# The second half's norm listed between the early up products, and the last down product ending by 256 tokens

## The chip, the cores and the metric

The kernel runs on one core of one Trainium2 chip, as one program. The metric is the device time of that program in microseconds (us): 2468.15 us as the median of 3 runs before the change (2466.43 to 2470.87). Engines are named as in the profile: PE is TensorE (matrix products), PEld its weight loads, DVE is VectorE, ACT is ScalarE, SP is the engine that issues all transfers here.

## The reference

Two decoder layers on 1024 tokens of width 1024, then a norm. All that matters here is the second part of a layer and the end:

```
for layer in range(DEPTH):
    ...
    x = x + mixed @ w_out[layer]
    h = rms_norm(x, norm_mlp[layer])
    x = x + jnp.square(jax.nn.relu(h @ w_up[layer])) @ w_down[layer]
return rms_norm(x, norm_final)
```

`rms_norm` divides each token by the root of the mean of its 1024 squares and multiplies by a gain per feature. The hidden width is 4096.

## The kernel before, in words

**Layout.** Activations lie transposed, features on the 128 partitions and tokens along the row: a tile is 128 features by 512 tokens (W), so a layer's x is 8 feature tiles times 2 token halves, `xs[k][hf]`. Q is 256 tokens. Every product is made of three float32r products of a rounded part h and a rest l (`ah`, `al`, `w..h`, `w..l`): ScalarE casts the h part, VectorE subtracts to get the l part (`split`, L316 and L318).

**Up product.** `h @ w_up` is done by Winograd's form of Strassen's scheme over the two feature halves and the two token halves: 7 products in place of 8 for each of 16 groups j of 256 hidden columns. Two of the seven need the first token half alone (`"11"` and `"21"`, operands `b11`, `b21`); the other five need differences of both halves (`"22"`, `"t1"` to `"t4"`, operands `b22`, `bt1` to `bt4`). `norm_up(hf)` norms one half and makes its operands: it saves 8 tiles of x to DRAM (`xm<-x`), sums the squares (`m0sq`; m1 in the second layer), has TensorE add them over the features (`m0ms`, L426 and L427), takes the reciprocal root on ScalarE (`m0rs`), and then, for each of four pairs p of feature tiles, makes the operands. For the second half (hf = 1) a pair costs VectorE two scaled copies (`mt<-x`, L448), four subtractions and five l parts, and ScalarE five casts.

`up_early` does the two first-half products of groups 0 to 9 (EARLY = 10): it splits the group's weights, multiplies, adds the products (`c<-m,psu`), squares the positive part and spills it. `up_rest(j)` does the other five products of such a group, with sums of the weights made on VectorE (`sums_of`: s1 to s4, each split as well); `up_all(j)` does all seven for groups 10 to 15.

**Order.** Nothing is issued in the order of the source. `op` lists each operation with a cost and its buffers, and the listing order is its number; generators that run through `weave` are listed alternately, by the given weights. `Program.order` then plays the list with its own costs: whenever an engine is free in that play, it takes the ready operation of the lowest number whose buffers can be had (not further ahead of the oldest open operation than a bound, 60 us of TensorE work). The order that comes out is fixed, and on the chip each engine works through its own list and waits where an input is late. Buffers are counted: 71 slots for tiles of 512 columns, 8 each for weight parts (`whi`, `wlo`), 4 for raw weights, 8 PSUM banks.

In listing order the second half's norm stands behind all of `up_early`, and `up_rest(0)` behind that norm.

**End of the last layer.** `down` multiplies the hidden tiles by `w_down` in seven products again. The last, `"22"`, is listed with `tail=4`: for j from 0 to 11 the four output tiles q take turns; for the last four j each q is brought to its end in turn (L1407 to L1409, 12 matmuls of 512 columns) and its result added to the second-half tile `xs[q][1]`. `norm_out` then squares the eight tiles, adds them (`finsq`), sums over features on TensorE (`finms`, one plain float32 product by a matrix of ones), takes the root (`finrs`, two ScalarE instructions), and eight times multiplies a tile by gain and root (`y<-x,colt,finrs`, L448) and stores it (L501). A branch of `norm_out` for a width of Q exists: there ScalarE multiplies by the gain beforehand, two tiles share one y of 128x2x256, four VectorE products by the root follow and four stores, with runs of 256 tokens in DRAM.

Of the kernel before, what the change touches and what calls it, by code (L numbers as in the profile page):

```python
# [15 lines left out]
OP = mybir.AluOpType  # L16
# [3 lines left out]
L = 2  # L20
# [4 lines left out]
KT = D // 128  # L25
NH = 2
W = 512
Q = 256
# [17 lines left out]
def weave(*parts):  # L46

    live = [[0, *p] if isinstance(p, tuple) else [0, p, 1] for p in parts]
    while live:
        part = min(live, key=lambda p: p[0] / p[2])  # L50
        part[0] += 1
        if next(part[1], live) is live:
            live.remove(part)
# [18 lines left out]
class Part:  # L72


    def __init__(self, buf, start, stop):
        self.buf, self.start, self.stop = buf, start, stop
        self.writers, self.readers = [], []

    @property
    def t(self):  # L80
# [35 lines left out]
class Program:  # L116
# [9 lines left out]
    def op(self, eng, cost, writes, reads, emit, table=None, join=False):  # L126
        engines = eng if isinstance(eng, dict) else {eng: cost}
        self.ops.append(Op(len(self.ops), engines, list(writes), list(reads), emit, table, join))
# [119 lines left out]
def trunk(ctx: ExitStack, tc: tile.TileContext, xT, wts, cols, trig, toep, lmask, ident_d, out):  # L248
    nc = tc.nc
    V, A, PE = nc.vector, nc.scalar, nc.tensor  # L250
# [15 lines left out]
    op = prog.op  # L266
# [23 lines left out]
    def c_mm(n):  # L290
        return max(107.0, 2.3 + n / 2.4)
# [10 lines left out]
    def tt(dst, a, b, kind, n=W, extra=()):  # L302

        op("DVE", c_tt(n), [dst[0]], [x[0] for x in (a, b) if x[0] is not None] + list(extra),
           lambda e: V.tensor_tensor(dst[1](), a[1](), b[1](), op=kind))  # L305

    def whole(b):
        return b, lambda: b.t
# [171 lines left out]
    def norm_out(xs, t0, width=W):  # L480
        r = rstd(xs[4:] + xs[:4], D, "fin", width=width)
        yield
        if width == Q:
            pairs = []
            for k in range(0, KT, 2):
                y = slot("y", shape=[128, 2, Q])
                for i in range(2):
                    op("ACT", c_act(Q) + 110, [y], [xs[k + i], colt], lambda e, y=y, i=i, k=k + i: A.activation(
                        y[:, i], xs[k].t, AF.Copy, scale=col(C_FIN + k)), join=True)
                pairs.append(y)  # L490
            for k, y in zip(range(0, KT, 2), pairs):
                tt(whole(y), whole(y), (r, lambda: r.t[:, None, :].to_broadcast([128, 2, Q])), OP.mult)
                op("SP", 730.0, [], [y], lambda e, k=k, y=y: nc.sync.dma_start(
                    out[k * 128:(k + 2) * 128, t0:t0 + Q].rearrange("(i p) t -> p i t", i=2), y.t))
                yield
            return
        for k in (4, 5, 6, 7, 0, 1, 2, 3):
            y = slot("y", width=width)
            stt(whole(y), whole(xs[k]), lambda k=k: col(C_FIN + k), whole(r), width)
            op("SP", 730.0, [], [y],  # L500
               lambda e, k=k, y=y: nc.sync.dma_start(out[k * 128:(k + 1) * 128, t0:t0 + width], y.t))  # L501
            yield
# [7 lines left out]
    def load_x(src, k, hf):  # L510
        x = slot(f"x{k}_{hf}")
        i, j = rows(k, hf)
        saved = src and src[k][hf]
        if saved:
            load(x, lambda: x.t, lambda: saved.t, 1 << 18, saved)
        else:
            load(x, lambda: x.t, lambda: xT[i, j], 1 << 18)
        return x
# [16 lines left out]
    xs, hs, rs, xsaved = table(), table(), {}, None  # L535
    first = [Group(j, f"w0h0{j}") for j in range(4)]
# [33 lines left out]
    for l in range(L):  # L570
# [621 lines left out]
        xs = table()  # L1192
# [6 lines left out]
        hf32, xmid = table(), table()  # L1199

        def norm_up(hf):


            for k in range(KT):
                d, x = Buf(f"xm{l}_{k}_{hf}", "dram", [128, W], F32), xs[k][hf]
                load(d, lambda d=d: d.t, lambda x=x: x.t, 1 << 18, x)
                xmid[k][hf] = d
            r = rstd([xs[k][hf] for k in range(KT)], D, f"m{l}", True)
            yield
            for p in range(4):  # L1210
                for k in (p, p + 4):
                    t = hf32[k][hf] = slot("mt")
                    stt(whole(t), whole(xs[k][hf]), lambda c=C_MLP + l * KT + k: col(c), whole(r))
                if hf == 0:
                    bo["11"].append(hilo(hf32[p][0], "b11", p < COUNT["kk"]))
                    bo["21"].append(hilo(hf32[p + 4][0], "b21"))
                else:
                    (b11, b12), (b21, b22) = hf32[p], hf32[p + 4]
                    bo["22"].append(hilo(b22, "b22"))
                    t3 = slot("t3")  # L1220
                    tt(whole(t3), whole(b22), whole(b12), OP.subtract)
                    bo["t3"].append(hilo(t3, "bt3"))
                    tt(whole(b12), whole(b12), whole(b11), OP.subtract)
                    bo["t1"].append(hilo(b12, "bt1"))
                    tt(whole(b22), whole(b22), whole(b12), OP.subtract)
                    bo["t2"].append(hilo(b22, "bt2"))
                    tt(whole(b21), whole(b21), whole(b22), OP.subtract)
                    bo["t4"].append(hilo(b21, "bt4"))
                yield
# [65 lines left out]
        def up_early():  # L1295

            for j in range(EARLY):
                grp = group_up(j)
                m1, c11 = slot("m1"), slot("c11")
                act(m1, product(grp.piece(0), "11", "sc"), AF.Copy)  # L1300
                m1s[j] = m1
                tt(whole(c11), whole(m1), whole(product(grp.piece(1), "21", "gemm")), OP.add)
                relu2(c11)
                spill("11", j, c11)
                yield
# [45 lines left out]
            operands(j, c11, c12, c21, c22)  # L1351

        weave((out_part(0, xs, (1,)), 8), (norm_up(0), 5))
        weave(up_early())
        weave(norm_up(1))
        for j in range(16):
            if j < EARLY:
                up_rest(j)
# [3 lines left out]
        xs = table()  # L1362
# [29 lines left out]
            tt(whole(sums[j]), a12, whole(sums[j]), OP.subtract)  # L1392
            return whole(sums[j])

        def down(n, weight, banks, into, first=True, tail=0):


            def operands(j):
                t = slot("al")
                load(t, lambda t=t: t.t, lambda d=ao[n][j]: d.t, 1 << 18, ao[n][j])  # L1400
                return *hilo(t, "a"), *parts(weight(j), f"w{l}d{n}{j}")

            def step(j, q, th, tl, wh, wl):
                ps = banks[q]

                def emit(e, cs=slice(q * 128, q * 128 + 128)):
                    PE.matmul(ps.t, lhsT=wh[:, cs], rhs=th.t, start=first and j == 0, stop=False, skip_group_check=True)  # L1407
                    PE.matmul(ps.t, lhsT=wh[:, cs], rhs=tl.t, start=False, stop=False, skip_group_check=True)  # L1408
                    PE.matmul(ps.t, lhsT=wl[:, cs], rhs=th.t, start=False, stop=j == 15, skip_group_check=True)  # L1409

                op("PE", 3 * c_mm(W), [ps], [wh, wl, th, tl], emit)
                if j < 15:
                    return
                for half, hf in into:
                    m = 4 * half + q
                    if xs[m][hf] is None:
                        xs[m][hf] = load_x(xmid, m, hf)
                    tt(whole(xs[m][hf]), whole(xs[m][hf]), whole(ps), OP.add)

            together = 16 - tail  # L1420
            for j in range(together):
                have = operands(j)
                for q in range(4):
                    step(j, q, *have)
                yield
            have = [operands(j) for j in range(together, 16)]
            for q in range(4) if tail else ():
                for j in range(together, 16):
                    step(j, q, *have[j - together])
                yield  # L1430

        def banks(*tags):
            return [bank("psd", t) for t in tags]

        some, rest = ("gemm", "gemm", "gemm", "acc"), ("sc", "sc", "tr", "tr")
# [4 lines left out]
        weave(down("t3", w_s3, chain, ((1, 1),), False))  # L1440
        weave(down("t4", lambda j: raw(j, 3, 1, "e")[0], chain, ((1, 0),), False))
        weave(down("21", lambda j: raw(j, 0, 1, "f")[0], banks(*rest), ((0, 0),)))
        final = down("22", w_s4, banks(*some), ((0, 1),), tail=4)
        if l + 1 < L:
            hs, rs, xsaved = table(), {}, table()
            after = [norm_in(l + 1, xs, hf, hs, rs, xsaved) for hf in range(NH)]
            weave((final, 16), (after[0], 9))
            weave(after[1])
            continue
        weave((final, 16), (norm_out([x[0] for x in xs], 0), 9))  # L1450
        weave(norm_out([x[1] for x in xs], W))

    loaded = "ln"
    for o in prog.order():
# [96 lines left out]
```

## Time and profile before

| | us |
|---|---|
| median of 3 runs | 2468.15 |
| profiled execution, time | 2466.34 |
| profiled execution, span of the trace | 2464.6 |
| TensorE busy | 2400.8 (97%) |
| VectorE busy | 1734.3 (70%) |
| ScalarE busy | 1209.8 (49%) |
| mean granted TensorE clock | 0.986 of full |

The span runs from the first to the last instruction of the trace; the program's own time is 1.7 us longer. A busy share says little here, since TensorE is called busy when its matmuls run slowly too; stretches with fewer matmuls per microsecond, or a lower granted clock (PEclk), are where time is lost.

### The profile page before, as it was taken

To read this page: it belongs to the slowest core of one execution; us is meant where nothing else is said; L and a number is where in the kernel's file an instruction comes from. 1 tells how busy PE (TensorE), PEld (TensorE's weight loads), DVE (VectorE), ACT (ScalarE), POOL (GpSimd) and SP (SyncE) were. 2 spreads that over 40 slices of the span, in tenths; PEclk is the share of its full clock that TensorE was granted. 3 is DMA by queue.
4 is the path that set the end of the run, shared out by engine and by line. 5 is a ranking of instruction groups with operands and counts; after the bars stand their busy time and mean duration, and the time that the engine had idled before them with its cause. 6 is when DMAs were issued, how large, how long until landed. Compare 5 with 4: busy or idle time off the path is not lost.

```text
span 2464.6 us, 35165 instructions
## 1 busy us (share of the span) xinstructions
PE 2400.8 (97%) x12522; PEld 2029.6 (82%) x12522; DVE 1734.3 (70%) x3403; ACT 1209.8 (49%) x2365; POOL 0.2 (0%) x4
## 2 busy tenths in 40 slices
PE   9999999999899999999999999999998999999997
PEld 7888898877678888888888989898776888888886
DVE  6366877788688667765744678788778875786565
ACT  7233346665554555444532333576555545554452
POOL 0000000000000000000000000000000000000000
PEclk9999999999899999999999999999998999999998
DMA  4011366843445469656520115668342654786562
GB/s 175 26 57 39 130 208 187 273 130 124 145 178 206 144 218 326 219 185 224 172 81 18 61 52 175 190 210 259 104 163 106 211 187 142 268 304 226 185 224 79
DMA packets 188656, 407.19 MB, mean 165 GB/s; under 512 B 22656, under 2 KB 23488, under 8 KB 188480
## 3 DMA queue, kind: packets, MB, share of 16 engines
q1 hardware_dynamic: 188480, 404.93, 49.0%
q8 instruction: 99, 1.62, 0.3%
q14 instruction: 77, 0.63, 0.1%
HBM read 291.37 MB, written 113.48 MB: 164 GB/s over the span
## 4 chain that ended last, share of the span: by engine, by line
PE 90%; DVE 4%; DMA 4%; ACT 2%; issue 1%; SPq 0%; DVEq 0%; ACTq 0%
PE psd L1409 8%; PE psd L1408 8%; PE psd L1407 8%; PE psu L1258 8%; PE psu L1257 8%; PE psu L1259 8%; PE sc L945 2%; PE pa L698 2%; PE pso L376 2%; PE pso L375 2%; PE pso L377 2%; PE pv L1108 2%; PE psv L400 1%; PE ptr L1095 1%; PE psva L400 1%; PE psv L401 1%
## 5 line engine op out<-in xcount | busy, mean ns | idle before, releaser
L318 DVE TENSOR_TENSOR al<-al,ah 128x512 fp32r<-128x512 f32 x224 | 152.6, 686 | 57.9 <-ACT ah L316 57.0
L316 ACT CAST ah<-al 128x512 fp32r<-128x512 f32 x224 | 137.0, 618 | 104.7 <-DMA al<-a 58.6
L961 ACT ACTIVATE sp<-sp,ls 128x256 f32<-128x256 f32 (+2 forms) x192 | 99.8, 522 | 16.7 <-DVE ls L950 16.3
L950 DVE CUSTOM_DVE_ANT_0 sp<-sc,tpt 128x256 f32<-128x256 f32 (+1 forms) x192 | 83.1, 439 | 32.1 <-PE sc L945 30.7
L945 PE MATMUL sc<-k,hd 128*128 128x256 f32 (+3 forms) x384 | 94.1, 356 | 7.7 <-DVE ls L950 3.5
L1240 ACT ACTIVATE c<-c 128x512 f32<-128x512 f32 x96 | 60.6, 631 | 35.1 <-DVE c L305 35.0
L1257 PE MATMUL psu<-bt3h,s3h 128*128 128x512 f32 x128 | 52.5, 410 | 23.5 <-ACT bt3h L316 21.8
L945 PEld LDWEIGHTS sc<-k,hd 128*128 128x128 f32 x384 | 60.5, 193 | 14.1 <-DVE ls L950 4.9
L316 ACT CAST pth<-ptr 128x512 fp32r<-128x512 f32 (+1 forms) x96 | 51.3, 552 | 39.0 <-PE ptr L1095 37.6
L1241 ACT ACTIVATE c<-c 128x512 f32<-128x512 f32 x108 | 68.3, 633 | 3.4
L318 DVE TENSOR_TENSOR ptl<-ptr,pth 128x512 fp32r<-128x512 f32 (+1 forms) x96 | 60.7, 641 | 10.4 <-ACT pth L316 9.4
L698 PEld LDWEIGHTS pa<-q,k 128*112 128x112 f32 (+3 forms) x512 | 62.0, 184 | 3.4
L698 PE MATMUL pa<-q,k 128*112 128x64 f32 (+3 forms) x512 | 61.2, 262 | 0.0
L305 DVE TENSOR_TENSOR x<-x,psd 128x512 f32<-128x512 f32 x64 | 41.4, 683 | 27.5 <-PE psd L1409 27.4
L1258 PE MATMUL psu<-bt3l,s3h 128*128 128x512 f32 x128 | 52.3, 408 | 2.2 <-DVE bt3l L318 2.2
L1095 PE MATMUL ptr<-ident,sp 128*128 128x128 f32 x352 | 53.6, 277 | 0.4 <-ACT sp L961 0.2
L305 DVE TENSOR_TENSOR x<-x,pso 128x512 f32<-128x512 f32 x64 | 43.4, 682 | 13.6 <-PE pso L377 12.9
L1258 PE MATMUL psu<-bt1l,s1h 128*128 128x512 f32 x128 | 51.8, 405 | 0.0
L1257 PE MATMUL psu<-bt1h,s1h 128*128 128x512 f32 x128 | 51.8, 404 | 0.0
L1259 PE MATMUL psu<-bt1h,s1l 128*128 128x512 f32 x128 | 51.8, 404 | 0.0
L1257 PEld LDWEIGHTS psu<-bt3h,s3h 128*128 128x128 f32 x128 | 24.6, 192 | 32.4 <-ACT bt3h L316 24.9
L1259 PE MATMUL psu<-bt3h,s3l 128*128 128x512 f32 x128 | 51.3, 400 | 0.0
(4978 smaller groups left out, 8097.0 us busy)
## 6 DMA issues: line engine op xcount, KB each, us to landing
al<-a SPq DMA_DIRECT2D x96, 256.0 KB
w0u<-in_wts_dram SPq DMA_DIRECT2D x42, 512.0 KB
w1u<-in_wts_dram SPq DMA_DIRECT2D x42, 512.0 KB
a<-c SPq DMA_DIRECT2D x76, 256.0 KB
al<-a0t SPq DMA_DIRECT2D x64, 256.0 KB
al<-a1t SPq DMA_DIRECT2D x64, 256.0 KB
hd<-q SPq DMA_DIRECT2D x48, 256.0 KB
a0t<-t SPq DMA_DIRECT2D x48, 256.0 KB
```

What stands on the lines that cost most here:

```text
L305: lambda e: V.tensor_tensor(dst[1](), a[1](), b[1](), op=kind))
L316: op("ACT", c_act(n), [hi[0]], [src[0]], lambda e: A.copy(hi[1](), src[1]()), join=join)
L318: lambda e: V.tensor_tensor(lo[1](), src[1](), hi[1]().bitcast(F32), op=OP.subtract), join=join)
L698: PE.matmul(pa[0:128 - b, c * 64:c * 64 + 64], lhsT=k[:, c * 128:c * 128 + 128 - b], rhs=by_half(q)[:, c, :, 1, :], start=True, stop=True)
L945: PE.matmul(ps[:, o:o + w], lhsT=q[:, q0:q0 + 128], rhs=k[:, keys], start=part == 0, stop=part == 1)
L961: op("ACT", c_act(w) + 190, [t, sum_], [t, m], lambda e, t=t, o=o, w=w, m=m, sum_=sum_: A.activation(t[:, o:o + w], t[:, o:o + w], AF.Exp, ...
L1257: PE.matmul(ps.t, lhsT=wh[:, cs], rhs=xh.t, start=first and k == 0, stop=False, skip_group_check=True)
L1258: PE.matmul(ps.t, lhsT=wh[:, cs], rhs=xl.t, start=False, stop=False, skip_group_check=True)
L1259: PE.matmul(ps.t, lhsT=wl[:, cs], rhs=xh.t, start=False, stop=k == 3, skip_group_check=True)
L1407: PE.matmul(ps.t, lhsT=wh[:, cs], rhs=th.t, start=first and j == 0, stop=False, skip_group_check=True)
L1408: PE.matmul(ps.t, lhsT=wh[:, cs], rhs=tl.t, start=False, stop=False, skip_group_check=True)
L1409: PE.matmul(ps.t, lhsT=wl[:, cs], rhs=th.t, start=False, stop=j == 15, skip_group_check=True)
```

## The change

The generator `norm_up(1)` is no longer listed behind `up_early()` but woven with it, in both layers, at weights 5 to 10: the sums of squares come behind group 0, the four pairs behind groups 2, 4, 6 and 8, and group 9 last.

In the last layer, the last four j of the last product are done in two rounds, first the tokens 0 to 255 of the half for all four q, then the tokens 256 to 511. Each round ends in its own additions to x (256 columns), and each round's 256 tokens have their own final norm, by the branch for a width of Q. `Part.of` makes a part of a buffer that has the buffer's earlier writers and readers. The loop over `load_x` finds all tiles loaded already by the first of the seven products.

```diff
+    @classmethod
+    def of(cls, buf, start, stop):
+        part = cls(buf, start, stop)
+        part.writers, part.readers = list(buf.writers), list(buf.readers)
+        return part
...
         weave((out_part(0, xs, (1,)), 8), (norm_up(0), 5))
-        weave(up_early())
-        weave(norm_up(1))
+        weave((up_early(), 10), (norm_up(1), 5))
...
-            def step(j, q, th, tl, wh, wl):
-                ps = banks[q]
+            def step(j, q, th, tl, wh, wl, end=None):
+                ps, ts = banks[q], slice(0, W)
+                if end:
+                    ps, ts = end[q][1], slice(end[q][1].start, end[q][1].stop)
...
+                    PE.matmul(ps.t, lhsT=wh[:, cs], rhs=th.t[:, ts], start=first and j == 0, stop=False, skip_group_check=True)
...
+                if end:
+                    x = end[q][0]
+                    tt(whole(x), whole(x), whole(ps), OP.add, Q)
                     return
...
-            for q in range(4) if tail else ():
-                for j in range(together, 16):
-                    step(j, q, *have[j - together])
-                yield
+            for end in ends if tail else ():
+                if end:
+                    (half, hf), = into
+                    for m in range(KT):
+                        ps = [Part.of(banks[m % 4], end.start, end.stop)] if m // 4 == half else []
+                        xend[end.start].append([Part.of(xs[m][hf], end.start, end.stop), *ps])
+                for q in range(4):
+                    for j in range(together, 16):
+                        step(j, q, *have[j - together], end and xend[end.start][4 * half:4 * half + 4])
+                    yield
...
-        final = down("22", w_s4, banks(*some), ((0, 1),), tail=4)
+        final = down("22", w_s4, banks(*some), ((0, 1),), tail=4, ends=(slice(0, Q), slice(Q, W)) if last else (None,))
...
-        weave(norm_out([x[1] for x in xs], W))
+        for t0 in 0, Q:
+            weave(norm_out([x[0] for x in xend[t0]], W + t0, Q))
```

## Rows read from the trace of the kernel before

**Rows 1.** The page, part 4: the chain that ended last, by engine.
```profile
PE 90%; DVE 4%; DMA 4%; ACT 2%; issue 1%; SPq 0%; DVEq 0%; ACTq 0%
```

**Rows 2.** View of waits, whole run: who waited for whom, total, times, longest.
```profile
PE psu L1257 <- ACT bt3h L316: 21.8, 6, 4.0
```

**Rows 3.** Busy time by stretch; first line names columns; x is instructions.
```profile
core 0: us, PE busy (x) PEld busy (x) DVE busy (x) ACT busy (x) POOL busy (x), PEclk, DMA share, GB/s
614.50:657.20 42.70, 42.66 (x186) 34.43 (x184) 20.94 (x33) 23.79 (x42) 0.00 (x0) 1.00 0.58 203
...
650.00:700.00 50.00, 38.23 (x134) 28.85 (x133) 43.31 (x71) 26.70 (x45) 0.00 (x0) 0.80 0.22 79
700.00:750.00 50.00, 50.00 (x222) 41.40 (x221) 41.56 (x68) 25.52 (x43) 0.00 (x0) 1.00 0.64 232
1865.00:1915.00 50.00, 37.83 (x136) 28.55 (x135) 42.68 (x70) 27.09 (x46) 0.00 (x0) 0.80 0.23 79
```

**Rows 4.** Timeline of TensorE, layer 0, end of `up_early`: start, length, instruction, idle before.
```profile
655.15 0.39 PE L426 MATMUL m0ms<-m0sh,ones_r 128*128 128x512 f32 x1
...
656.77 0.39 PE L1259 MATMUL psu<-b21h,w0u91l 128*128 128x512 f32 x1
661.18 0.79 PE L1257 MATMUL psu<-bt3h,s3h 128*128 128x512 f32 x1 [4.02 <-ACT bt3h L316]
...
669.43 0.63 PE L1257 MATMUL psu<-bt1h,s1h 128*128 128x512 f32 x1
669.86 0.63 PE L1258 MATMUL psu<-bt1l,s1h 128*128 128x512 f32 x1
```

**Rows 5.** Timeline of VectorE, layer 0: `up_early`, then the second half's norm.
```profile
613.72 0.69 DVE L318 TENSOR_TENSOR m0sl<-m0sq,m0sh 128x512 fp32r<-128x512 f32 x1
...
624.95 0.69 DVE L305 TENSOR_TENSOR c<-m,psu 128x512 f32<-128x512 f32 x1 [1.79 <-PE psu L1259]
...
628.00 0.69 DVE L318 TENSOR_TENSOR w0u80l<-w0u,w0u80h 128x512 fp32r<-128x512 f32 x1 [1.75 <-ACT w0u80h L316]
630.48 0.69 DVE L305 TENSOR_TENSOR c<-m,psu 128x512 f32<-128x512 f32 x1 [1.79 <-PE psu L1259]
...
657.81 2.07 DVE L448 SCALAR_TENSOR_TENSOR mt<-x,colt,m0rs 128x512 f32<-128x512 f32 x3
...
663.41 0.68 DVE L305 TENSOR_TENSOR mt<-mt 128x512 f32<-128x512 f32 x1
664.01 0.68 DVE L318 TENSOR_TENSOR bt2l<-mt,bt2h 128x512 fp32r<-128x512 f32 x1
...
684.78 0.68 DVE L318 TENSOR_TENSOR bt4l<-mt,bt4h 128x512 fp32r<-128x512 f32 x1
```

**Rows 6.** Timeline of TensorE, layer 0: where group 3 of `up_early` begins.
```profile
616.46 0.40 PE L1257 MATMUL psu<-b,w0u30h 128*128 128x512 f32 x1
```

**Rows 7.** Timeline of TensorE: matmuls of 256 columns, six from first to last.
```profile
58.88 0.28 PE L400 MATMUL psv<-w0h032h,n_0h 128*128 128x256 f32 x1
...
59.59 0.40 PE L375 MATMUL psq<-n_1h,w0h013h 128*128 128x512 f32 x1
```

**Rows 8.** Groups by line, shapes apart: VectorE at 256 columns (total us, mean ns).
```profile
L305 DVE TENSOR_TENSOR q<-q,tot 128x256 f32<-128x256 f32 x96 | 40.6, 423 | 6.5 <-PE pa L715 6.3
```

**Rows 9.** Timeline of the end, all engines.
```profile
2449.69 0.39 PE L1409 MATMUL psd<-ah,w1d2215l 128*128 128x512 f32 x1
2450.16 1.31 ACT L312 ACTIVATE finsq<-x 128x512 f32<-128x512 f32 x2 [4.13 <-DVE x L305]
2452.36 2.08 PE L432 MATMUL finms<-finsq,ones 128*128 128x512 f32 x2 [2.29 <-DVE finsq L305]
2454.48 0.69 ACT L312 ACTIVATE finrs<-finms,epst 128x512 f32<-128x512 f32 x1 [3.01 <-PE finms L432]
2455.86 5.39 DVE L448 SCALAR_TENSOR_TENSOR y<-x,colt,finrs 128x512 f32<-128x512 f32 x8 [3.55 <-ACT finrs L312]
2456.64 4.97 SPq L501 DMA_DIRECT2D out_dram<-y  x8
```

More of the change, by code (lines that the diff above doesn't have):

```diff
@@ L1393, in w_s4, with down @@
             return whole(sums[j])
-        def down(n, weight, banks, into, first=True, tail=0):
+        def down(n, weight, banks, into, first=True, tail=0, ends=(None,)):
             def operands(j):
@@ L1401, in operands @@
                 return *hilo(t, "a"), *parts(weight(j), f"w{l}d{n}{j}")
-            def step(j, q, th, tl, wh, wl):
-                ps = banks[q]
+            def step(j, q, th, tl, wh, wl, end=None):
+                ps, ts = banks[q], slice(0, W)
+                if end:
+                    ps, ts = end[q][1], slice(end[q][1].start, end[q][1].stop)
                 def emit(e, cs=slice(q * 128, q * 128 + 128)):
[L1407 to L1411, printed above, removed]
+                    PE.matmul(ps.t, lhsT=wh[:, cs], rhs=th.t[:, ts], start=first and j == 0, stop=False, skip_group_check=True)
+                    PE.matmul(ps.t, lhsT=wh[:, cs], rhs=tl.t[:, ts], start=False, stop=False, skip_group_check=True)
+                    PE.matmul(ps.t, lhsT=wl[:, cs], rhs=th.t[:, ts], start=False, stop=j == 15, skip_group_check=True)
+                op("PE", 3 * c_mm(ts.stop - ts.start), [ps], [wh, wl, th, tl], emit)
                 if j < 15:
+                    return
+                if end:
+                    x = end[q][0]
+                    tt(whole(x), whole(x), whole(ps), OP.add, Q)
                     return
@@ L1442, in trunk @@
         weave(down("21", lambda j: raw(j, 0, 1, "f")[0], banks(*rest), ((0, 0),)))
-        final = down("22", w_s4, banks(*some), ((0, 1),), tail=4)
-        if l + 1 < L:
+        xend = {0: [], Q: []}
+        last = l + 1 == L
+        if last:
+            for m in range(4):
+                if xs[m][1] is None:
+                    xs[m][1] = load_x(xmid, m, 1)
+        final = down("22", w_s4, banks(*some), ((0, 1),), tail=4, ends=(slice(0, Q), slice(Q, W)) if last else (None,))
+        if not last:
             hs, rs, xsaved = table(), {}, table()
```

## The prediction, made before the change was run

> **What bounds the kernel now.** I read the chain of waits first: 90% of it is TensorE [rows 1], so time is won only where TensorE stands still or runs slowly. The view of waits then says where: its largest own wait is for ScalarE's `bt3h`, 21.8 us in 6 waits [rows 2]; these are operands of the second half's norm. The table of stretches shows the full price: from 700 to 750 TensorE starts 222 matmuls in 50 us, one per 0.225 us; from 650 to 700 it starts 134, from 1865 to 1915 136 [rows 3]. Missing are 88 and 86, so 19.8 + 19.4 = 39.2 us over the two layers. This is more than the waits because the granted clock in these stretches is 0.80 of full [rows 3]: after the 4.02 us gap matmuls follow each other at 0.43 us (669.43 to 669.86) [rows 4], the 1.2 GHz level, half the other.
>
> The timelines say why. The squares of the second half are ready when `m0sl` ends at 614.4 [rows 5], but `m0ms` starts at 655.15 [rows 4]: its number stands behind all early products, and TensorE always has one of those. VectorE starts the norm's pairs at 657.81 and ends at 685.46 [rows 5], while TensorE has nothing else it may do. And in the 42.7 us before, VectorE was busy for 20.9 and ScalarE for 23.8 [rows 3].
>
> **The change, part by part.** *Step 1: the norm moves.* `m0ms` now has a number behind group 0 and is taken as soon as its input is there. Two matmuls, two ScalarE instructions and eight stores of x move with it; the stores wait only for x, which is long ready, and no compute waits for them. Price nothing; were the 8 stores to hold SP's queue, weights would come late, but splits run three groups ahead of their use.
>
> *Step 2: does VectorE have room?* The norm's work from 657.81 to 685.46 is 44 instructions with one foreign one of 0.60 between: 27.0 us, or 6.75 per pair (instructions start every 0.60, 663.41 to 664.01) [rows 5]. An early group lasts 5.53 us on TensorE (624.95 to 630.48) and costs VectorE one addition and two splits [rows 5], 1.8 us. So in the woven part, two groups and one pair are 3.6 + 6.75 = 10.35 us of VectorE against 11.06 of TensorE: 94%. It fits, barely. The idle time from 614.5 to 657.2 is 42.7 - 20.9 = 21.8 us [rows 3], against 27.0 wanted; the missing 5 us come out of the weight sums of `up_rest(0)` and `(1)`, which VectorE now does ahead in this stretch and which move behind the norm. A group of `up_rest` is the next customer; from 700 to 750 VectorE is busy 41.6 of 50 [rows 3], so it has 17% to catch up with. ScalarE: 23.8 us plus 20 casts of some 0.62 are 36 of 42.7: no bound.
>
> *Step 3: what is late next.* Two places. First, the opening: once the root is there all four pairs are ready at once, and pair 0 stands ahead of the splits of group 3, which TensorE reaches at 616.46 [rows 6]. The root comes between 611 and 616 (before, `m0sl` began at 613.72 [rows 5] with the nine splits of groups 1 to 5, 0.60 each, ahead of it that now stand behind; 655.15 to 657.81 is the way from `m0ms` to the first copy [rows 4, 5]). So group 3's splits wait for between nothing and a pair, 6.75 us; I take 2 us of standstill. Second, the change to `up_rest(0)`: nine VectorE instructions (sums and splits, 5.4 us) are wanted there and some 6 us are left for them after the last pair: I take no wait. A standstill of some 2 us can cost as much again: `finms`, after 2.29 us without work, takes 2.08 us for two matmuls [rows 9], a slow level; 15 matmuls at 0.43 instead of 0.225 are 3.1 us. So I leave 5 us per layer standing of 19.6, with ends of 0 (no wait at all) and 12 (the opening's full pair, a slow spell and 2 us at the transition). Gain: 39.2 - 10 = 29.2 us, ends 39.2 and 15.
>
> The Trainium skill ("TensorE: Matmul & The Clock Gate", section on the 16 sub-arrays, at its queue depths) says that ScalarE and VectorE take their instructions strictly first in, first out. By it a pair's late instruction holds every split listed behind it, also those whose inputs are there. No row of before shows the price, since the norm stands behind all splits there; what it would do is the last rival below.
>
> *Step 4: 256 columns in the last product.* 48 matmuls of 512 columns become 96 of 256. At 256 columns six take 0.71 us (58.88 to 59.59) [rows 7], 0.118 each, weights loaded for each as here: 96 x 0.118 - 48 x 0.226 = +0.5 us.
>
> *Step 5: the end.* Before, from the start of the last matmul (2449.69) to the span's end (2464.6) it is 14.9 us, of which the eight last products on VectorE take 5.39 and begin only at 2455.86; the last store is issued by 2461.61 and 3.0 us remain [rows 9]. After, counted from the last matmul's start: the first 256 tokens' squares are summed already, but their `finms` has a higher number than the second round's matmuls and goes behind them, at 0.1, for about 0.5 (half of it would be 1.04 at the slow level [rows 9]); two root instructions of 0.42 (the row of 256 columns [rows 8], taken for ScalarE as well): 1.45. Four products of 128x512 at 0.60, 0.08 for the last's length: 4.0. In between the last x tile is added and squared (2.0 at most), but its addition to the sum has the higher number, so VectorE takes it after those four: 4.4. Then `finms` at the slow level 1.04, the root 0.85, four products 2.5: 8.8; and from there 3.35 us as before (2461.25 to 2464.6): 12.2. That is 2.7 less than 14.9; with step 4, 2.2 us gained. If the sum's addition goes first, the second chain runs beside the first and 2.4 us more are gained (4.6). If a store in runs of half the length took twice the time, four stores at 0.62 each (4.97 us for 8 [rows 9]) cost 2.5 more: 0.3 lost. I take 2.2.
>
> *Sum.* The profiled execution took 2466.34 (span 2464.6 and 1.7 around it): 2466.3 - 29.2 - 2.2 = 2434.9. The median of the runs is 1.8 above that execution, so I give 2437.
>
> **Rivals.** *A, all of it goes:* no standstill stays in either layer and the end gains 4.6: 2468.2 - 43.8 = 2424. For it: the sums of work fit. Against: 94% leaves VectorE nothing where three engines pass operands to and fro.
>
> *B, VectorE's debt comes back:* the pairs are done early, but the sums for `up_rest(0)` and `(1)`, 16 instructions before 657 (33 in the stretch [rows 3], less 8 additions and 9 splits), come too late, and TensorE starves at the transition instead, at a slow clock. 5 to 10 us of lateness and its slow spell leave about half of the loss standing: 2468.2 - 19.6 - 2.2 = 2446. For it: 21.8 us of room against 27.0. Against: `up_rest` leaves 17% free.
>
> *C, the planner keeps the order:* numbers change but buffers keep the norm late. Only the end moves: 2466. Against: the norm's operands are held at the start of `up_rest` in any case.
>
> *D, slower: the pairs starve the early products.* In VectorE's list a pair stands ahead of the next splits. If passing to and fro with ScalarE stretches the 10.35 us over the 11.06, TensorE stands still some 2 us in each of the four pairs, each time with a slow spell of 3 us, and once more at the transition: 25 us per layer against 19.6 saved. With the end that is 2468 + 10.8 - 2.2 = 2477. It decides from four such stops in each layer; fewer only cut the gain. For it: 94%. Against: a slow TensorE lets VectorE catch up, and at 657.81 to 684.78 pairs run without gaps on VectorE [rows 5].
>
> **How the numbers follow.** Forecast (2429 to 2443) 0.50; A 0.15; B 0.22; C 0.05; D 0.08. A measurement of this kernel tells about 0.2% (4.9 us) from no change. Faster by more: forecast, A, B, less a little of B that ends near 2463: 0.86. Within: C and that rest: 0.06. Slower: D, 0.08. The range runs from A's 2424 to 2456, where B reaches with the full 12 us per layer and 5 more; C and D and an edge of A are left out.
>
> **What would show it.** In the changed profile `m0ms` starts by 616, not 655, and `bt3h` is gone from TensorE's waits; the first 50 us after the last early product hold some 215 matmuls or more, at a clock near 1.00. VectorE is busy over 90% from 611 to 657. A standstill near group 3 in each layer of about 2 us bears out step 3; one at each pair is D; one at the first `s2h` or `s3h` is B. At the end, matmuls 0.118 us apart, four plus four products of VectorE, the last addition to the sum of squares behind the first four (else the 4.6), and 12.2 us from the last matmul of the product to the end. The prediction is wrong if VectorE or ScalarE cannot carry the pairs beside the early groups.

## The result, and the profile after

The changed kernel takes 2427.4 us (median of 4 runs, 2424.93 to 2435.95) against 2469.5 before: a ratio of 0.983 (95% interval 0.980 to 0.986), some 42 us less. The forecast was 2437, with 2424 for the case that no standstill is left at all and the end gains 4.6. The profiled execution is the slowest of the four, 2435.95 with a span of 2434.2; in it TensorE also lost time in parts that the change doesn't touch (its last matmul starts at 2422.59, in the repetition `after_again` at 2416.39), so stretches are compared below, not spans.

The stretches that answer to [rows 3], in the changed kernel; columns as there:

```profile
614.50:657.20 42.70, 42.70 (x187) 34.81 (x187) 40.83 (x67) 32.98 (x58) 0.00 (x0) 1.00 0.46 151
650.00:700.00 50.00, 50.00 (x221) 41.30 (x220) 43.96 (x72) 26.51 (x45) 0.00 (x0) 1.00 0.53 180
700.00:750.00 50.00, 50.00 (x222) 41.42 (x221) 41.11 (x67) 25.05 (x42) 0.00 (x0) 1.00 0.57 210
1865.00:1915.00 50.00, 50.00 (x223) 41.39 (x222) 42.59 (x70) 24.49 (x41) 0.00 (x0) 1.00 0.54 188
```

Where 134 and 136 matmuls started, 221 and 223 do, at the full clock. From 614.5 to 657.2, beside the early products, VectorE is busy for 40.8 of 42.7 us, where it was for 20.9: its idle time took the norm.

TensorE around the sum of squares and at the end of `up_early`, against [rows 4]:

```profile
613.63 0.39 PE L433 MATMUL m0ms<-m0sh,ones_r 128*128 128x512 f32 x1
...
620.98 0.40 PE L1264 MATMUL psu<-b,w0u30h 128*128 128x512 f32 x1
...
659.44 0.39 PE L1266 MATMUL psu<-b21h,w0u91l 128*128 128x512 f32 x1
659.66 0.39 PE L1264 MATMUL psu<-bt2h,s2h 128*128 128x512 f32 x1
...
661.02 0.39 PE L1264 MATMUL psu<-bt3h,s3h 128*128 128x512 f32 x1
```

`m0ms` starts at 613.6 instead of 655.2, and the first product with the second half starts 0.22 us after the last early one, where 4.41 us lay, 4.02 of them idle. Group 3 begins at 620.98.

VectorE at the opening, against [rows 5]:

```profile
611.73 0.69 DVE L325 TENSOR_TENSOR m0sl<-m0sq,m0sh 128x512 fp32r<-128x512 f32 x1
612.33 0.69 DVE L325 TENSOR_TENSOR w0u30l<-w0u,w0u30h 128x512 fp32r<-128x512 f32 x1
...
614.74 0.68 DVE L325 TENSOR_TENSOR w0u50l<-w0u,w0u50h 128x512 fp32r<-128x512 f32 x1
...
616.28 2.07 DVE L455 SCALAR_TENSOR_TENSOR mt<-x,colt,m0rs 128x512 f32<-128x512 f32 x3
...
624.38 0.68 DVE L325 TENSOR_TENSOR w0u51l<-w0u,w0u51h 128x512 fp32r<-128x512 f32 x1
...
655.01 0.68 DVE L325 TENSOR_TENSOR bt4l<-mt,bt4h 128x512 fp32r<-128x512 f32 x1
```

While the root is on its way (612 to 616) five splits get done, those of groups 3 and 4 and the first of group 5; the pairs then run from 616.3 to 655.7, with early groups' splits and additions between them.

The end, against [rows 9]:

```profile
2422.59 0.28 PE L1417 MATMUL psd<-ah,w1d2215l 128*128 128x256 f32 x1
2422.71 0.60 PE L439 MATMUL finms<-finsq,ones 128*128 128x256 f32 x2
2424.15 0.42 DVE L312 TENSOR_TENSOR finsq<-finsq 128x256 f32<-128x256 f32 x1 [0.27 <-ACT finsq L319]
2424.50 4.90 DVE L312 TENSOR_TENSOR y<-y,finrs 128x512 f32<-128x512 f32 x8
2424.63 0.70 PE L439 MATMUL finms<-finsq,ones 128*128 128x256 f32 x2 [1.33 <-DVE finsq L312]
2425.21 5.01 SPq L500 DMA_DIRECT2D out_dram<-y  x8
```

From the start of the last matmul (2422.59) to the span's end (2434.2) it is 11.6 us, before 14.9.

### The profile page after: what moved, and what is told of

The parts are those of the page before. It is cut to its first block, busy times and chain, and to the rows that moved or that the text cites. A ratio compares the mean times of both kernels' runs of the same rounds, so it can differ in the third digit from the quotient of the medians.

```text
span 2434.2 us, 35321 instructions
## 1 busy us (share of the span) xinstructions
PE 2390.8 (98%) x12572; PEld 2029.5 (83%) x12572; DVE 1733.8 (71%) x3414; ACT 1217.5 (50%) x2391; POOL 0.2 (0%) x4
## 4 chain that ended last, share of the span: by engine, by line
PE 91%; DMA 4%; DVE 2%; ACT 2%; SPq 0%; issue 0%; DVEq 0%; ACTq 0%
PE psd L1415 8%; PE psd L1416 8%; PE psd L1417 8%; PE psu L1264 8%; PE psu L1265 8%; PE psu L1266 8%; PE sc L952 2%; PE pa L705 2%; PE pso L383 2%; PE pso L382 2%; PE pso L384 2%; PE pv L1115 1%; PE psv L407 1%; PE psq L382 1%; PE psv L408 1%; PE psv L409 1%
## 5 line engine op out<-in xcount | busy, mean ns | idle before, releaser
L312 DVE TENSOR_TENSOR x<-x,psd 128x512 f32<-128x512 f32 (+1 forms) x68 | 41.8, 652 | 25.3 <-PE psd L1417 25.1
L312 DVE TENSOR_TENSOR x<-x,pso 128x512 f32<-128x512 f32 x64 | 43.4, 681 | 15.2 <-PE pso L384 14.7
L1122 ACT COPY pvt<-pv 64x256 f32<-64x256 f32 x80 | 29.6, 370 | 47.0 <-PE pv L1115 45.5
L713 DVE COPY_PREDICATED at<-lmt,pa 126x256 f32<-126x256 uint8 (+1 forms) x64 | 32.8, 512 | 25.1 <-PE pa L705 24.4
L1266 PE MATMUL psu<-b22h,s4l 128*128 128x512 f32 x128 | 49.8, 389 | 0.0
```

The source lines that it names most:

```text
L1266: PE.matmul(ps.t, lhsT=wl[:, cs], rhs=xh.t, start=False, stop=k == 3, skip_group_check=True)
```

## The experiments

Ten kernels, each beside the kernel before on the same chip. The theory after the result: the standstill of 39.2 us is gone in full, since VectorE had the room; the end gives some 3 us. Rivals: the end gives more; any early place in the list would have done; pairs need numbers of their own.

**The two parts apart, and the whole again.** `norm_only` is the kernel before with one line changed, `end_only` the changed kernel with that line put back:

```diff
-        weave(up_early())
-        weave(norm_up(1))
+        weave((up_early(), 10), (norm_up(1), 5))
```

> The norm of the second half woven with the early up products, the end as before. The theory that the whole gain comes from TensorE's standstill behind the norm expects 39 us less than before (19.8 and 19.4 in the two layers), no slower stretch of TensorE from 600 to 700, and the end as before: 14.9 us from the last matmul of the product to the span's end. The rival, by which the end gives a good part, expects 34 us less or fewer.

> The last product ending by 256 tokens, the norm listed as before. The theory expects 2 to 3 us less than before, within what a measurement can tell; in the trace 11.6 us from the last matmul to the span's end where before has 14.9, and 0.5 us more for the narrow matmuls. The rival (the end gives a good part of the gain) expects 6 us less or more.

> The changed kernel once more, beside the others. The theory that the standstill is gone in full and the end gives 2 to 3 us expects 41 to 42 us less than before; the forecast, by which a quarter of the loss stays, expects 31.

| kernel | median, us | before, us | ratio, 95% interval |
|---|---|---|---|
| norm_only | 2433.7 | 2471.4 | 0.9844 (0.9825 to 0.9862) |
| end_only | 2466.7 | 2471.4 | 0.9987 (0.9976 to 0.9998) |
| after_again | 2431.2 | 2471.4 | 0.9834 (0.9820 to 0.9848) |

The norm alone gives 1.56%, 38.6 us; the end 0.13%, 3 us with an interval from nearly none to 6; the whole 41. The parts add up. In the trace of `norm_only` TensorE starts 222 matmuls from 650 to 700 (below), and its end has the length of before: 2410.17 to 2425.4, 15.2 us. `end_only` has its last matmul at 2454.64 and ends at 2465.9, 11.3 us, and waits as before.

`norm_only`, stretch:

```profile
650.00:700.00 50.00, 50.00 (x222) 41.29 (x221) 43.31 (x71) 26.01 (x44) 0.00 (x0) 1.00 0.54 187
```

`end_only`, the view of the tile `bt3h`: who waited for it, us and times:

```profile
  PE psu L1264: 21.9, 6
...
  PE psu L1265: 2.2, 6
```

So 24.1 us of the 39 are standstill. The other 15 are matmuls that take longer: the kernel before is busy for 38.23 us from 650 to 700 with 134 matmuls [rows 3], which at 0.225 us each are 30.2, so 8 us in the first layer and 7 in the second. In the first layer some 30 matmuls run at the 1.2 GHz level after a standstill, 0.43 us apart, which is 6 of the 8; the first matmul after a gap takes longer still (0.79 us against 0.63 [rows 4]).

**What of the norm had to move.** `root_early` lists only the stores, squares and root behind group 0; the pairs are numbered behind all early groups, as before the change:

```diff
-        weave((up_early(), 10), (norm_up(1), 5))
+        early, second = up_early(), norm_up(1)
+        next(early)
+        next(second)
+        weave(early)
+        weave(second)
```

> The changed kernel, but only the stores, squares and root of the second half are listed behind group 0; its four pairs stand behind all early groups again. The theory that what held the norm was the number of its one TensorE sum expects the whole gain (within 4 us of the changed kernel, some 40 less than before): VectorE has 21.8 us idle among the early groups and takes the pairs there, since they are ready. The rival, by which the pairs need numbers among the early groups, expects half of the standstill back, 20 us less than before.

Measured: 2430.7 against 2472.1, 0.9833 (0.9816 to 0.9850), the same gain. Its stretch from 650 to 700 and three instructions of its VectorE:

```profile
650.00:700.00 50.00, 50.00 (x221) 41.30 (x220) 44.43 (x73) 26.36 (x44) 0.00 (x0) 1.00 0.49 168
```

```profile
617.35 2.07 DVE L455 SCALAR_TENSOR_TENSOR mt<-x,colt,m0rs 128x512 f32<-128x512 f32 x3
...
656.08 0.68 DVE L325 TENSOR_TENSOR bt4l<-mt,bt4h 128x512 fp32r<-128x512 f32 x1
656.68 0.68 DVE L325 TENSOR_TENSOR s2l<-s,s2h 128x512 fp32r<-128x512 f32 x1
```

The pairs run in the same stretch (617 to 656) though they are numbered behind every early group: with the root there, they fill what VectorE has idle. Of what `root_early` moves, only `m0ms` had been late: its squares were ready at 614.4 before the change too, and the first copy followed 2.7 us after `m0ms` [rows 4, 5]. So what held the norm was the number of two matmuls.

**How late the norm may come.** `norm_late6` weaves it with the groups 6 to 9 only, `norm_late8` with 8 and 9. The lines of `norm_late8`; `norm_late6` has 6 and 4 in place of 8 and 2:

```diff
-        weave((up_early(), 10), (norm_up(1), 5))
+        early = up_early()
+        weave(itertools.islice(early, 8))
+        weave((early, 2), (norm_up(1), 5))
```

> The changed kernel, but the norm is woven with the groups 6 to 9 only. Group 6 begins some 33 us after group 0, so pairs run from about 636 and end about 668, 11 us after the last early product instead of 28 (before) or none. If the loss goes with that lateness, 19.6 x 11 / 28 = 8 us per layer come back: 25 us less than before. If any place among the early groups is enough, nothing comes back: 41 less than before.

> The same with the groups 8 and 9 only: pairs from about 647 to 677, 20 us after the last early product. If the loss goes with the lateness, 14 us per layer come back: 13 us less than before. If any place is enough: 41 less.

Measured against 2472.1: 2450.4, 0.9908 (0.9891 to 0.9926), 22.7 us less, where 25 were expected; and 2457.8, 0.9941 (0.9923 to 0.9959), 14.6 less, where 13 were. So the gain falls with the time at which the pairs can start; "any early place" is out. The pairs run from 642 to 672 and from 651 to 680. The stretches (in this order `norm_late6`, `norm_late8`), and the wait of each:

```profile
650.00:700.00 50.00, 43.51 (x180) 35.08 (x179) 49.41 (x81) 28.89 (x48) 0.00 (x0) 0.93 0.38 137
```

```profile
650.00:700.00 50.00, 39.81 (x154) 30.82 (x153) 48.40 (x80) 28.82 (x49) 0.00 (x0) 0.90 0.28 99
```

```profile
659.16 0.39 PE L1265 MATMUL psu<-bt1l,s1h 128*128 128x512 f32 x1
666.03 0.79 PE L1266 MATMUL psu<-bt1h,s1l 128*128 128x512 f32 x1 [6.49 <-DVE s1l L325]
```

```profile
675.02 0.80 PE L1264 MATMUL psu<-bt3h,s3h 128*128 128x512 f32 x1 [4.19 <-ACT bt3h L323]
```

In `norm_late6` TensorE does not wait for the norm: it waits 6.5 us for `s1l`, a weight sum of `up_rest(0)` that the pairs pushed back. This is the wait of rival B, with VectorE busy for 49.4 of 50 us. The rule of lateness, which took TensorE to wait for the pairs, came near in its number for another reason; 42 matmuls fewer than 222 are 9.5 us per layer. In `norm_late8` `bt3h` is late again (3.91 us at 661, 4.19 at 675).

**Does the order on VectorE matter?** `norm_first` lists all pairs right behind group 0:

```diff
-        weave((up_early(), 10), (norm_up(1), 5))
+        early = up_early()
+        next(early)
+        weave(norm_up(1))
+        weave(early)
```

> The changed kernel, but all four pairs are listed right behind group 0, ahead of the additions and splits of the groups 1 to 9. If order on VectorE matters (its list is worked through in order, a pair ahead of a split delays it), the 27 us of pairs stand ahead of what TensorE needs next and it stands still 10 to 20 us in each layer: 0 to 20 us less than before. If room on VectorE is all that counts, the order of pairs and splits changes nothing: 41 less than before.

Measured: 2454.9, 0.9929 (0.9906 to 0.9952), 17.6 us less. TensorE of `norm_first`, VectorE at the end of that wait, then the stretch:

```profile
627.92 0.40 PE L1266 MATMUL psu<-b11h,w0u50l 128*128 128x512 f32 x1
636.14 0.79 PE L1264 MATMUL psu<-b21h,w0u41h 128*128 128x512 f32 x1 [7.81 <-DVE c L312]
636.73 0.63 PE L1265 MATMUL psu<-b21l,w0u41h 128*128 128x512 f32 x1
637.15 0.63 PE L1266 MATMUL psu<-b21h,w0u41l 128*128 128x512 f32 x1
```

```profile
634.20 0.69 DVE L325 TENSOR_TENSOR bt4l<-mt,bt4h 128x512 fp32r<-128x512 f32 x1
...
635.40 0.68 DVE L312 TENSOR_TENSOR c<-m,psu 128x512 f32<-128x512 f32 x1
```

```profile
600.00:650.00 50.00, 40.87 (x165) 32.43 (x164) 45.66 (x75) 31.44 (x55) 0.00 (x0) 0.90 0.31 97
```

It stands 7.8 us for an addition `c` on VectorE that empties a PSUM bank and stands behind the pairs. The same stretch of the changed kernel holds 219 matmuls, so 54 are missing here, 12 us in this layer. So the mechanism of rival D is real, at the price of 23 us in all (41 less 17.6), but not at the place where the change put the pairs.

**A shorter end.** `end_woven` lists the first 256 tokens' norm between the second round's matmuls; `end_split` lists only its root there, and both roots ahead of all eight products; `root_end` is `root_early` with the end of `end_split`. The lines of `end_split`:

```diff
-        weave((final, 16), (norm_out([x[0] for x in xs], 0), 9))
-        for t0 in 0, Q:
-            weave(norm_out([x[0] for x in xend[t0]], W + t0, Q))
+        weave((itertools.islice(final, 16), 16), (norm_out([x[0] for x in xs], 0), 9))
+        next(final)
+        one = norm_out([x[0] for x in xend[0]], W, Q)
+        next(one)
+        weave(final)
+        two = norm_out([x[0] for x in xend[Q]], W + Q, Q)
+        next(two)
+        weave(one)
+        weave(two)
```

> As the changed kernel, but the final norm of the first 256 tokens is listed between the second round's matmuls, so that its sum over features, its products and its four stores run beside them. If the end is bound by what follows the last matmul (eight products and eight stores), it is 1.5 to 2.5 us shorter than in the changed kernel: about 9.5 us from the last matmul to the span's end, 0.5 us more in between for the sum of squares. If the way to the last store alone sets it (addition, squares, root, product, store), nothing changes.

> The changed kernel, but at the end both roots are listed ahead of the first 256 tokens' products: the first root between the second round's matmuls, its products whenever VectorE is free under them, the second round's sum of squares ahead of what is left of them. If the end is bound by eight products and eight stores behind the last matmul, half of them are gone from there: 9.5 to 10 us from the last matmul of the product to the span's end, 11.6 in the changed kernel, 1 to 2 us less in all. If the stores alone set it, 11 us as with the first sort of weaving.

> Both: the root alone listed early, with the end of the run before it. If the two are independent, as the changed kernel's 41 us less and 1 to 2 us more: 42 to 44 us less than before.

Measured, in this order: 2427.3 against 2471.4, 0.9822 (0.9806 to 0.9837); 2429.1 against 2468.6, 0.9836 (0.9822 to 0.9850); 2427.9 against 2468.6, 0.9835 (0.9820 to 0.9850). None can be told from the changed kernel; `root_end` is 41 us below the kernel before, where 42 to 44 were expected. In the traces the ends take 11.1 us (`end_woven`, 2411.81 to 2422.9) and 11.0 (`end_split`, 2416.46 to 2427.5; `root_end` 11.0 as well) against 11.6: some 0.5 gained where 1.5 to 2.5 and 1 to 2 were expected. `end_split`:

```profile
2416.46 0.28 PE L1417 MATMUL psd<-ah,w1d2215l 128*128 128x256 f32 x1
...
2418.66 0.42 DVE L312 TENSOR_TENSOR finsq<-finsq 128x256 f32<-128x256 f32 x1
2419.13 0.70 PE L439 MATMUL finms<-finsq,ones 128*128 128x256 f32 x2 [2.39 <-DVE finsq L312]
...
2420.82 2.50 DVE L312 TENSOR_TENSOR y<-y,finrs 128x512 f32<-128x512 f32 x4 [1.75 <-ACT finrs L319]
2422.74 0.98 SPq L500 DMA_DIRECT2D out_dram<-y  x2
```

Here the eight products and their stores are no longer the bound: the transfers pause from 2421 to 2422 (DMA share 0.00). The 11.0 us are the way from the last matmul to the second root, 4.4 us, with two of the first round's products still between the squares on VectorE; then 2.9 us from there to the end of the last store's issue, with four products; and 3.8 us from that to the span's end, where it was 3.0 before the change [rows 9]. The theory was wrong in two points: only two of the eight products, not half of them, went from behind the last matmul, and the chain through the second root is nearly as long as the end was.

## Why the prediction came out as it did

The change was forecast to gain 31 us (2468.2 to 2437) and gained 42, and 41 in the repetition. The time alone does not tell the forecast from rival A: 2427.4 lies between A's 2424 and the forecast's lower edge 2429, and the 2431.2 of `after_again` lies inside the forecast's own range. The traces do: the 10 us of standstill and slow matmuls that the forecast left in place are not there. That the time fell into the stated range is due to the range's lower end, which was A, and not to step 3.

- **What bounds, and the 39.2 us.** Right: `norm_only` gains 38.6 by its ratio, and its matmuls from 650 to 700 are back to 222. Reading missing matmuls rather than waits was the step that gave the size: 24 us are waits, the rest slower matmuls.
- **Step 1.** Right and stronger than said: `root_early` shows that the pairs needed no new numbers; with `m0ms` early they go where VectorE is idle.
- **Step 2.** Right: VectorE had the room, by a little. It is busy 40.8 of 42.7 us, 96%, where 94% was worked out. The room that was missing came from the weight sums, as said: of their 16 instructions before 657.2, four are left there. `norm_late6` shows what happens with less room.
- **Step 3.** Failed in size. I left 5 us per layer standing, for group 3's splits behind the first pair and for the slow clock that follows. Neither came: TensorE lost nothing. VectorE used the wait for the root for five splits (612.33 to 615.4), and those of group 3 were done at 613.6, ahead of the first pair and 7 us ahead of TensorE, which reached group 3 at 620.98 and not at 616.46. The planner also set later splits between the instructions of the pairs, such as `w0u51l` at 624.38. Step 1 had said that splits run three groups ahead of their use, and step 3 did not use it. My own range for this wait began at nothing; I took 2 us of it and then added the clock's price, which made 10 us in two layers, nearly the whole distance to the measured time. That price was not certain either: in `end_split` a wait of 2.39 us was followed by two matmuls of 256 columns in 0.70 us at a granted clock of 0.96 (2419 to 2420), where half of the 2.08 us of [rows 9] would be 1.04. The transition to `up_rest(0)` took no wait, as said.
- **Step 4.** Right: 0.12 us per matmul of 256 columns (2422.35 to 2422.59 in the end is two of them).
- **Step 5.** Near in the sum, wrong in its parts: 11.6 us against 12.2 forecast. The addition to the sum of squares goes ahead of the first four products (2424.15 against 2424.50), the case for which I gave 2.4 us more gain, so 9.8 us. The products did come early: the eight of them run as one chain of 4.90 us and end 6.8 us after the start of the last matmul, where that case gives 6.4. What is longer is the way from there to the span's end: 4.8 us, where I took 3.35 from the kernel before, and from the last store's issue 4.0, not 3.0. The transfers are wholly busy from 2427 to 2432, so the stores and not the products set the end, and they are slower: from 2428 to 2431 341 GB/s, in the kernel before, with runs twice as long in DRAM, from 2458 to 2461 380. I had named slower stores, at twice the time, and then left them out of the sum. That the runs' length is the reason is not shown by a run of its own; three other kernels agree (`after_again` 340 and `end_only` 338 GB/s with the short runs, `norm_only` 382 with the long ones, each over 3 us with the transfers wholly busy).
- **Rivals.** Of A, for which I gave 0.15, the first half came true, that no standstill stays; the end did not gain its 4.6 but some 3. B and D are mechanisms that this kernel has, but the change stays clear of both: B's wait appears in `norm_late6`, D's in `norm_first`. C is out: `m0ms` moved by 41.5 us.

Stretches of stores, changed kernel, then the kernel before:

```profile
2428.00:2431.00 3.00, 0.00 (x0) 0.00 (x0) 1.39 (x3) 0.00 (x0) 0.00 (x0) 0.50 1.02 341
```

```profile
2458.00:2461.00 3.00, 0.00 (x0) 0.00 (x0) 3.00 (x5) 0.00 (x0) 0.00 (x0) 0.50 1.02 380
```

## What to carry to other kernels

In a list worked by number, look for the one cheap instruction on the busiest engine that opens a long chain on the others: here two matmuls, numbered behind 10 groups of products, cost 39 us in two layers. Price such a hole by the matmuls missing against a full stretch, not by its waits, and check that the idle time of the chain's engine holds the chain, since the gain falls as soon as it does not. Where a range for a wait begins at nothing, ask what the engine does meanwhile before taking the middle.

## What the runs showed of the hardware

The lower granted clock made most of 15 of the 39 us: in the kernel before, after standstills of 3 to 4 us, matmuls started 0.43 us apart, the 1.2 GHz level, and a standstill of 7.8 us in `norm_first` was followed by the same (636.73 to 637.15). Stores of the same size, 256 KB, came out 10% slower with runs of 1 KB than with 2 KB (341 against 380 GB/s with the transfers wholly busy).
